# Moving the per-layer input's product from the last stage into the RWKV preparation

## The chip, the core and the metric

One core of a Trainium2 chip runs the whole program. The metric is the device time of one execution in microseconds (us). The profile names the core's engines PE (matrix products; PEld is its weight loads), DVE (vector), ACT (scalar and table functions), POOL (GpSimd) and SP (which here only starts transfers, on the queue the profile calls SPq). On-chip data lies in SBUF, matrix products land in PSUM banks of 128 x 512 numbers, and everything else is in DRAM.

## The reference

One encoder layer over 1024 tokens of width 1024. Only what the change touches is spelled out:

```python
h = rms_norm(x, norm_mix);  proj = h @ w_in            # q, k, v | r, k, v, decay, rate, gate | branch gates
attn = windowed_gqa(q, k, v)                            # 128-token bands
rw = rwkv7_time_mix(...)                                # two scans, forward and backward
x = x + (gate0 * (attn @ w_up_attn) + gate1 * (rw @ w_up_rwkv)) @ w_out
x = x + square(relu(rms_norm(x) @ w_ff1)) @ w_ff2
hp = rms_norm(x, norm_ple)
x = x + (p @ w_ple) * sigmoid(hp @ w_ple_gate)          # p: 1024 x 256, an input
```

`p @ w_ple` needs no result of the layer: `p` (1024 x 256) and `w_ple` (256 x 1024) are both inputs.

## The kernel before

Every fp32 operand of a large product is split into a high part (a rounding cast on ACT, L187) and a low part (the remainder, a subtraction on DVE or POOL, L188), and each product is three matrix instructions: high by high, high by low, low by high (`mm3`, L222; `mm3_steps`, L210, the same one at a time). A weight slab goes through `load_w` (L193): it is loaded in two halves into a staging tile (tag `w_st`, two buffers), each half is cast on ACT, and its remainder is taken on POOL; the parts lie in `w_hi` and `w_lo`, two buffers each.

The stages, in time order:

1. Norm, transposes and the q, k, v columns (to about 105 us). Near its end the transposed keys go to DRAM by POOL's queue (`kT_d`, L362).
2. The RWKV preparation (`with ExitStack() as s1`, L476, about 105 to 375 us). It finishes two column slabs (z12 and z13: decay, rate and gate inputs), and then loops over four pairs of heads `p`. Each turn projects k, r and v (48 matrix instructions each; `shifted`, L510, averages neighbouring tokens: ACT copies, a sum on POOL at L522, a scaled sum on DVE at L523), forms four low-rank products (`lora`, L541, a 128-row and a 64-row instruction for each half), and runs a long DVE and ACT chain to the scan's operands, which go to DRAM at L681 and L682. The "bonus" of turn p is finished by PE during turn p+1 (`add_bonus`, L574): two banks of sums over `rk`, and eight transposes of v. In the last turn the branch gates' products (`gates`, L280) are put between the low-rank products.
3. Attention (about 380 to 510 us), with what is left of the gates as filling. It reads `kT`, which POOL loads from DRAM at L463, ahead of the preparation's first work on POOL.
4. The scan by chunks, the output product, the two feed-forward products in a seven-product scheme (L1448, L1698).
5. The last stage (L1756), over eight tiles of 128 tokens: for each half of 512 columns, six matrix instructions for `p @ w_ple` into one PSUM bank (`pwps`, L1763) and 24 for `hp @ w_ple_gate` into another (`plps`), then a tanh on ACT (L1779) and two DVE instructions (L1780, L1781). During tile k the operands of tile k+1 are made: `p` is loaded, transposed (two instructions) and split; the normed x is transposed (eight instructions) and split.

A planner orders each engine's instructions ahead of the run. It gives the earlier instruction of the program precedence among those whose operands and buffers are free; only the few marked `keep_in_program_order` are tied. A tile takes a buffer of its tag once an earlier tile's last reader is done. On the chip every engine and queue then runs its list in that order.

Of the kernel before, what the change touches and what calls it, by code (L numbers as in the profile page):

```python
# [9 lines left out]
F32 = mybir.dt.float32  # L10
# [127 lines left out]
def block_kernel(ctx: ExitStack, tc: tile.TileContext, I: dict, out: bass.AP):  # L138
# [21 lines left out]
    x1_d = DR.tile([T, DM], F32, name="x1_d")  # L160

    hid_d = {r: DR.tile([FF // P // 2, P, 512], F32, name="hid_" + r) for r in ("A11", "A12", "A22", "S1", "S2", "S3", "S4")}
    kT_d = DR.tile([P, 2, 2, T], F32R, name="kT_d")
    qT_d = DR.tile([NT, P, NH, P], F32R, name="qT_d")
    va_d = DR.tile([T, P], F32, name="va_d")
# [293 lines left out]
            pass  # L459
    sQ.close()  # L460

    kT = PY.tile([P, 2, 2, T], F32R, name="kT", tag="yk")
    nc.gpsimd.dma_start(kT, kT_d)  # L463
    gmask = const("gmask", [P, ND, P])
    pc = G.tile([P, NPC], F32, name="pc")
    nc.sync.dma_start(pc, I["pc"])
# [9 lines left out]
    with ExitStack() as s1:  # L476
# [64 lines left out]
        def lora(d, p, i, bias_col):  # L541

            th = A1.tile([P, T], F32, name="th", bufs=2)
            for h in range(2):
                ps = PX.tile([P, 512], F32, name="px", tag="px", bufs=6)
                cs_, hs = slice(p * P, (p + 1) * P), slice(512 * h, 512 * h + 512)
                nc.tensor.matmul(ps, wlr_h[i][:, d, cs_], lr[i][:, hs], start=True, stop=False)
                nc.tensor.matmul(ps, wlr_l[hrows[i], d, cs_], lr[i][hrows[i], hs], start=False, stop=True)
                nc.scalar.activation(out=th[:, 512 * h:512 * h + 512], in_=ps, func=AF.Tanh, scale=0.5, bias=hb[:, bias_col:bias_col + 1])
            return th  # L550

# [48 lines left out]
        def proj_with(c0, hooks):  # L600
# [9 lines left out]
                    i += 1  # L610
            return pss

        bonus = None
        for p in range(NP):
            if bonus:
                next(bonus)
            kz = shifted(O_RWKV + 512 + p * P, 4 + p)
            rz = shifted(O_RWKV + p * P, p, pin=p > 0)

            kk = A1.tile([P, T], F32, name="kk", bufs=1)  # L620
            ri = A1.tile([P, T], F32, name="ri", tag="sm", bufs=1)
# [17 lines left out]
            for d in range(ND):  # L639
# [33 lines left out]
                nc.vector.scalar_tensor_tensor(out=bk[:, :, bs, :], in0=ch(ta), scalar=0.5, in1=Ei, op0=ALU.mult, op1=ALU.mult)  # L673
                nc.vector.tensor_tensor(out=bk[:, :, ks, :], in0=ch(kd), in1=Ei, op=ALU.mult)
                if d == 0:
                    rk = A1.tile([P, T], F32, name="rk", bufs=1)
                    nc.vector.tensor_scalar_mul(rk, kd, col("r_k", p))
                else:
                    nc.vector.scalar_tensor_tensor(out=rk, in0=kd, scalar=col("r_k", NP + p), in1=rk, op0=ALU.mult, op1=ALU.add)
                    nc.vector.tensor_tensor(out=rk, in0=rk, in1=rz, op=ALU.mult)  # L680
# [952 lines left out]
        nc.vector.tensor_tensor(out=xv, in0=xv, in1=src_, op=ALU.add)  # L1633


    wpv = I["w_ple"].rearrange("(k p) n -> p k n", p=P)
    wgv = I["w_ple_gate"].rearrange("(k p) n -> p k n", p=P)
    wg, loads = [None] * 4, []

# [28 lines left out]
    def ple_load(k):  # L1668
        pt = F2.tile([P, PLE], F32, name="pt", tag="sst", bufs=3)
        nc.sync.dma_start(pt, I["p"][tok(k)[1], :])  # L1670
        return pt

    def ple_p(pt):

        pp = F2.tile([P, 2, 2, P], F32R, name="pp", tag="tmp", bufs=2)
        transpose_split(PH, "acc", pt, lambda q, w: pp[:, 0, q:q + w, :], lambda q, w: pp[:, 1, q:q + w, :], nk=2, bufs=8)
        return pp[:, 0], pp[:, 1]

    def ple_x(xs):

# [5 lines left out]
    for ip, (lr_, rr_, bs, fresh) in enumerate(PRODS):  # L1686
        if fresh:
            banks[bs] = [acc() for _ in range(4)]
        for p in range(NPR):
            if ip == 0 and p < NPRE:  # L1690
                sh, sl, th_, tl_ = pre[p]
            else:
                sh, sl = parts_of(F2, ("sh", "sl"), fetch(F2, hid_d[lr_][p], "sst", 3), NR2)
                th_, tl_ = parts_of(F2, ("th", "tl"), right_of(p, rr_), NR2)
            for i in range(4):
                isl = slice(i * P, (i + 1) * P)
                for j, (x_, y_) in enumerate(((sh, th_), (sh, tl_), (sl, th_))):
                    nc.tensor.matmul(banks[bs][i], x_[:, isl], y_, start=fresh and p + j == 0,  # L1698
                                     stop=p == NPR - 1 and j == 2, skip_group_check=True)
            if ip == 0 and p == NPRE - 1:  # L1700
                sRF.close()
                sFP.close()
                PXX = pool(sX, "x1", side="right")
                X = [PXX.tile([P, 4, DM], F32, name=f"X{e}") for e in range(2)]
                c1 = pool(sC1, "c1", side="right").tile([P, 4, 512], F32, name="c1r")
                t2r = pool(sT2, "t2", side="right").tile([P, NPR, 512], F32, name="t2r")
                t1r = pool(sT1, "t1", side="right").tile([P, NPR, 512], F32, name="t1r")
            if ip == 0 and 0 <= p - (NPR - T1EARLY - NPRE) < NPRE:
                q = p - (NPR - T1EARLY - NPRE)
                nc.sync.dma_start(b11[:, q], w2_block(q, "B11"))  # L1710
            if ip == 0 and p >= NPR - T1EARLY:
                t1_of(p - (NPR - T1EARLY))
            if ip == 1 and p % 2 == 0:
                e, i = divmod(p // 2, 4)
                t = torder[4 * e + i]
                nc.sync.dma_start(X[e][:, i, :], x1_d[t * P:(t + 1) * P, :])
            if ip == 3 and p < 12:
                add_to(*((0, 1), (1, 1), (1, 0))[p // 4], p % 4, c1[:, p % 4])
            if ip > 3 and p % 3 == 1:
                load_next()  # L1720
            if ip == 6:
                if p == 4:
                    pt, xs = ple_load(0), ple_norm(0)
                    ple_scale(0, *xs)
                if p == 9:
                    nxt = [ple_p(pt), ple_x(xs[0])]
        for i in range(4):
            b_ = banks[bs][i]
            if ip == 0:
# [4 lines left out]
        if ip == 3:  # L1734
            sB11.close()
            PLEW = pool(sP, "plew")
            gainp = PLEW.tile([P, DM], F32, name="gainp", bufs=1)
            nc.sync.dma_start(gainp, I["gains"][2:3, :].partition_broadcast(P))
            wp = [PLEW.tile([P, 2, DM], F32R, name=f"wp{i}", bufs=1) for i in range(2)]
            loads += [(wp[0][:, k:k + 1], wp[1][:, k:k + 1], wpv[:, k:k + 1]) for k in range(2)]  # L1740
            ple_gate_w(PLEW, 0)
        if ip == 4:
            sT1.close()
# [7 lines left out]
            PXS = pool(sT2, "plex", bufs=2, side="right")  # L1751
    while loads:
        load_next()


    for k in range(NT):  # L1756
        (pph, ppl), hp = nxt
        nxt = [None, None]
        xv, rows = tok(k)
        for n in range(2):  # L1760
            nsl = slice(512 * n, 512 * n + 512)
            pw = acc(name="pwps")
            mm3(pw, [(pph[:, j, :], ppl[:, j, :], wp[0][:, j, nsl], wp[1][:, j, nsl]) for j in range(2)])  # L1763
            th = F2.tile([P, 512], F32, name="pth", tag="tst", bufs=3)
            ps_ = acc(name="plps")
            steps = mm3_steps(ps_, [(hp[j // 4][0][:, j % 4, :], hp[j // 4][1][:, j % 4, :],
# [1 line left out]
            for m in range(2):  # L1768
                if k + 1 < NT and (n, m) == (0, 0):
                    xs = ple_norm(k + 1)  # L1770
                    pt = ple_load(k + 1)
                    ple_scale(k + 1, *xs)
                if k + 1 < NT and (n, m) == (0, 1):
                    nxt[0] = ple_p(pt)
                if k + 1 < NT and (n, m) == (1, 1):
                    nxt[1] = ple_x(xs[0])
                for _ in range(12):
                    next(steps, None)
            nc.scalar.activation(out=th, in_=ps_, func=AF.Tanh, scale=0.5)  # L1779
# [36 lines left out]
```

## Time and profile before

| | us |
|---|---|
| median of 3 runs | 1818.32 (1815.65 to 1825.78) |
| the profiled execution | 1818.63 |
| its span, first to last instruction | 1816.9 |
| PE busy in the span | 1714.2 (94%) |
| DVE, ACT, POOL busy | 1135.8, 883.1, 321.7 |
| mean granted PE clock | 0.977 of full speed |
| matrix instructions of `p @ w_ple` in the last stage | 96, from 1677.9 us on |
| last instruction of PE | begins at 1811.4 us |

A row of the timeline gives the start, the length, the engine, the line of the kernel, the operation and, in brackets, how long the engine was idle before it and on whom it waited. Matrix instructions overlap, so the step from start to start, not the length, is what one costs. A row of the groups ends with "busy us, mean ns | idle us before, and who ended it".

### The profile page before, as it was taken

What the parts mean: (1) busy time and instruction counts of PE and PEld (TensorE: products, weight loads), DVE (VectorE), ACT (ScalarE), POOL (GpSimd) and SP (SyncE); (2) the same over time, 40 slices, a digit from 0 to 9 for tenths busy, and PEclk for the clock granted to TensorE, in tenths of its full rate; (3) what the DMA queues carried; (4) which work ended last, traced back from release to release, by engine and by line L of the source; (5) the groups of instructions that cost most, each with busy time, mean ns of one, the idle gap of its engine ahead of it and who ended that gap; (6) DMA issues with size and microseconds to landing.
All of it is one profiled execution on the core that took longest, in us unless ns stands there. A gap on an engine that the chain in (4) does not pass through costs nothing. (4 is left out here: it accounts for less than half of the span.)

```text
span 1816.9 us, 29645 instructions
## 1 busy us (share of the span) xinstructions
PE 1714.2 (94%) x11288; PEld 1376.5 (76%) x11288; DVE 1135.8 (63%) x1931; ACT 883.1 (49%) x1624; POOL 321.7 (18%) x265
## 2 busy tenths in 40 slices
PE   7999888989999898988889989999999999999998
PEld 7977666766677777776667867888888888888887
DVE  5646777745845646575564277766766887685442
ACT  5546666547764555455542154544444444454221
POOL 3454544532132112112142000000000000000000
PEclk9999999999999999989999989999999999999999
DMA  5462344674377474576576214444456984574111
GB/s 198 99 183 81 117 145 145 197 202 115 98 201 203 141 196 148 158 199 197 175 225 198 93 47 151 151 152 161 143 163 214 324 262 122 187 221 135 62 41 47
DMA packets 281998, 285.96 MB, mean 157 GB/s; under 512 B 49408, under 2 KB 195712, under 8 KB 281728
## 3 DMA queue, kind: packets, MB, share of 16 engines
q1 hardware_dynamic: 273600, 270.76, 48.3%
q0 software_dynamic: 7824, 12.59, 2.5%
q8 instruction: 89, 1.46, 0.3%
q10 hardware_dynamic: 432, 0.73, 0.1%
q14 instruction: 53, 0.43, 0.1%
HBM read 203.26 MB, written 80.74 MB: 156 GB/s over the span
## 5 line engine op out<-in xcount | busy, mean ns | idle before, releaser
L188 POOL TENSOR_TENSOR wlo<-wst,whi 128x512 fp32r<-128x512 f32 x100 | 149.6, 1508 | 313.1 <-ACT whi L187 262.4
L1698 PE MATMUL ff2ps<-tl,sh 128*128 128x512 f32 x448 | 174.4, 389 | 0.1
L1698 PE MATMUL ff2ps<-th,sl 128*128 128x512 f32 x448 | 174.3, 389 | 0.0
L1698 PE MATMUL ff2ps<-th,sh 128*128 128x512 f32 x448 | 173.9, 389 | 0.0
L175 POOL TENSOR_TENSOR rstd<-ms,neghalf 128x1 f32<-128x1 f32 x24 | 13.3, 554 | 792.9 <-DVE ms L173 792.9
L187 ACT CAST sh<-sst 128x512 fp32r<-128x512 f32 x109 | 67.8, 622 | 99.5 <-PE ff2ps L1698 50.3
L188 DVE TENSOR_TENSOR sl<-sst,sh 128x512 fp32r<-128x512 f32 x109 | 75.1, 689 | 47.4 <-ACT sh L187 47.2
L1698 PEld LDWEIGHTS ff2ps<-tl,sh 128*128 128x128 f32 x448 | 84.1, 188 | 18.2 <-DVE tl L188 0.5
L1698 PEld LDWEIGHTS ff2ps<-th,sh 128*128 128x128 f32 x448 | 84.0, 188 | 17.7 <-ACT th L187 0.3
L1698 PEld LDWEIGHTS ff2ps<-th,sl 128*128 128x128 f32 x448 | 84.1, 188 | 17.5
L187 ACT CAST whi<-wst 128x512 fp32r<-128x512 f32 x100 | 60.7, 619 | 47.5 <-DMA wst<-in_w_in_dram 16.1
L187 ACT CAST w1h<-w1st 128x512 fp32r<-128x512 f32 x48 | 28.5, 621 | 101.1 <-DMA w1st<-in_w_ff_dram 64.1
L188 DVE TENSOR_TENSOR w1l<-w1st,w1h 128x512 fp32r<-128x512 f32 x48 | 31.9, 688 | 52.2 <-ACT w1h L187 52.2
L208 PE MATMUL gps<-rm,bkp 128*128 128x256 f32 x256 | 62.4, 386 | 1.3 <-ACT tm L1061 0.8
L1034 DVE TENSOR_TENSOR gm<-gps,gmask 128x512 f32<-128x512 f32 x64 | 43.7, 685 | 29.5 <-PE gps L208 29.5
L218 PE MATMUL gmm<-hh,wlo 128*128 128x512 f32 x144 | 59.3, 412 | 0.0
L214 PE MATMUL gmm<-hh,whi 128*128 128x512 f32 x144 | 59.2, 411 | 0.0
L216 PE MATMUL gmm<-hl,whi 128*128 128x512 f32 x144 | 59.2, 411 | 0.0
L1086 DVE COPY Wt<-wps 64x512 f32<-64x512 f32 x16 | 10.9, 680 | 71.3 <-PE wps L208 71.3
L208 PEld LDWEIGHTS gps<-rm,bkp 128*128 128x128 f32 x256 | 47.2, 189 | 10.9 <-issue 1.4
L226 PE MATMUL mm<-hh,whi 128*128 128x512 f32 x128 | 51.5, 402 | 3.3 <-ACT z L520 3.3
L188 DVE TENSOR_TENSOR w1l<-ssum,w1h 128x512 fp32r<-128x512 f32 x64 | 43.0, 688 | 16.9 <-ACT w1h L187 16.9
(409 smaller groups left out, 5056.8 us busy)
## 6 DMA issues: line engine op xcount, KB each, us to landing
wst<-in_w_in_dram SPq DMA_DIRECT2D x92, 256.0 KB, 3.5
tst<-in_w_ff_dram SPq DMA_DIRECT2D x80, 256.0 KB, 4.0
w1st<-in_w_ff_dram SPq DMA_DIRECT2D x32, 512.0 KB, 5.2
hid_S<-h SPq DMA_DIRECT2D x64, 256.0 KB, 2.1
sst<-hid_S SPq DMA_DIRECT2D x64, 256.0 KB, 2.8
hid_A<-h SPq DMA_DIRECT2D x48, 256.0 KB, 2.0
sst<-hid_A SPq DMA_DIRECT2D x45, 256.0 KB, 3.9
ra_d<-ra SPq DMA_DIRECT2D x8, 1024.0 KB, 4.5
```

The costliest lines, as they stand in the source:

```text
L175: nc.gpsimd.tensor_tensor(out=r, in0=ms, in1=neghalf.broadcast_to([P, width]), op=ALU.pow)
L187: a = nc.scalar.copy(hi, src)
L188: b = (lo_eng or nc.vector).tensor_tensor(out=lo, in0=src, in1=hi.bitcast(F32), op=ALU.subtract)
L208: tc.keep_in_program_order(nc.tensor.matmul(*a, **kw))
L214: mm(ps, ah, bh, start=(i == 0), stop=False)
L216: mm(ps, ah, bl, start=False, stop=False)
L218: mm(ps, al, bh, start=False, stop=(i == n - 1))
L226: nc.tensor.matmul(ps, ah, bh, start=(i == 0), stop=False)
L1034: nc.vector.tensor_tensor(out=gm[d][:, s % NB, 4 * h:4 * h + 4, :], in0=ps.rearrange("p j q t -> p (j q) t"), in1=gmask[:, d, :].unsqueeze ...
L1086: nc.vector.tensor_copy(Wt[own[0], 0], wp[own[0]])
L1698: nc.tensor.matmul(banks[bs][i], x_[:, isl], y_, start=fresh and p + j == 0, stop=p == NPR - 1 and j == 2, skip_group_check=True)
```

## The change

The product `p @ w_ple` is computed in the preparation, stored to a DRAM tensor `pw_d` and loaded again in the last stage. `ple_in(g)` loads, transposes and splits four tiles of `p`; `ple_product(g, n)` makes four token tiles' half of 512 columns: a slab of `w_ple` through `load_w`, 24 matrix instructions, four copies on ACT, four stores. `ple_in(0)` stands ahead of the loop; two products follow the k and r projections of turn 0, one (with `ple_in(1)`) follows the r projection of turn 1, one that of turn 2. The `p` tiles are staged in `w_st`, the split `p` lies in the buffer of `kT` (tag `yk`), so `kT` is loaded in turn 3; half of the copies go through `gth`, the tag of the bonus sums' second half. To make room, `rk` shares one buffer with `vt` and `bv`. In `lora`, both 128-row instructions now come first, then both 64-row ones.

```diff
+    pw_d = DR.tile([T, DM], F32, name="pw_d")
...
-    kT = PY.tile([P, 2, 2, T], F32R, name="kT", tag="yk")
-    nc.gpsimd.dma_start(kT, kT_d)
...
         def lora(d, p, i, bias_col):
...
-            for h in range(2):
-                ps = PX.tile([P, 512], F32, name="px", tag="px", bufs=6)
-                cs_, hs = slice(p * P, (p + 1) * P), slice(512 * h, 512 * h + 512)
+            pss = [PX.tile([P, 512], F32, name="px", tag="px", bufs=6) for _ in range(2)]
+            for ps, hs in zip(pss, hss):
                 nc.tensor.matmul(ps, wlr_h[i][:, d, cs_], lr[i][:, hs], start=True, stop=False)
+            for ps, hs in zip(pss, hss):
                 nc.tensor.matmul(ps, wlr_l[hrows[i], d, cs_], lr[i][hrows[i], hs], start=False, stop=True)
+            for h, ps in enumerate(pss):
                 nc.scalar.activation(out=th[:, 512 * h:512 * h + 512], in_=ps, func=AF.Tanh, ...)
...
+        pT = PY.tile([P, NT, 2, 2, P], F32R, name="pT", tag="yk")
+        wpv = I["w_ple"].rearrange("(k p) n -> p k n", p=P)
+        def ple_in(g):
+            for i in range(4):
+                t = 4 * g + i
+                pt = PW.tile([P, PLE], F32, name="pt", tag="w_st", bufs=2)
+                nc.sync.dma_start(pt, I["p"][t * P:(t + 1) * P, :])
+                tp = PX.tile([P, 2, P], F32, name="ptp", tag="px", bufs=6)
+                for k in range(2):
+                    nc.tensor.transpose(tp[:, k, :], pt[:, k * P:(k + 1) * P], ident)
+                split(pT[:, t, 0], pT[:, t, 1], tp)
+        def ple_product(g, n):
+            nsl = slice(512 * n, 512 * n + 512)
+            hi, lo = load_w(PW, "w", wpv[:, :, nsl], 512, parts=2)
+            for i in range(4):
+                t = 4 * g + i
+                ps = PX.tile([P, 512], F32, name="pwps", tag="px", bufs=6)
+                mm3(ps, [(pT[:, t, 0, k, :], pT[:, t, 1, k, :], hi[:, k, :], lo[:, k, :]) for k in range(2)])
+                o_ = (A1, PW)[i % 2].tile([P, 512], F32, name="pws", tag=("pws", "gth")[i % 2], bufs=2)
+                nc.scalar.copy(o_, ps)
+                nc.sync.dma_start(pw_d[t * P:(t + 1) * P, nsl], o_)
+        ple_in(0)
...
             kz = shifted(O_RWKV + 512 + p * P, 4 + p)
+            if p == 0:
+                ple_product(0, 0)
             rz = shifted(O_RWKV + p * P, p, pin=p > 0)
+            if p == 0:
+                ple_product(0, 1)
+            elif p < 3:
+                if p == 1:
+                    ple_in(1)
+                ple_product(1, p - 1)
+            else:
+                kT = PY.tile([P, 2, 2, T], F32R, name="kT", tag="yk")
+                nc.gpsimd.dma_start(kT, kT_d)
...
-                    rk = A1.tile([P, T], F32, name="rk", bufs=1)
+                    rk = A1.tile([P, T], F32, name="rk", tag="vt", bufs=1)
...
+    def ple_load(k, n):
+        pw = F2.tile([P, 512], F32, name="pw", tag="sst", bufs=3)
+        nc.sync.dma_start(pw, pw_d[tok(k)[1], 512 * n:512 * n + 512])
+        return pw
...
-            pw = acc(name="pwps")
-            mm3(pw, [(pph[:, j, :], ppl[:, j, :], wp[0][:, j, nsl], wp[1][:, j, nsl]) for j in range(2)])
+            pw = npw
+            if 2 * k + n + 1 < 2 * NT:
+                npw = ple_load(*divmod(2 * k + n + 1, 2))
...
-                if k + 1 < NT and (n, m) == (0, 1):
-                    nxt[0] = ple_p(pt)
```

The old loads of `w_ple` and `p` in the last two stages, and their splits, are gone as well.

More of the change, by code (lines that the diff above doesn't have):

```diff
@@ L543, in lora @@
             th = A1.tile([P, T], F32, name="th", bufs=2)
-            for h in range(2):
-                ps = PX.tile([P, 512], F32, name="px", tag="px", bufs=6)
-                cs_, hs = slice(p * P, (p + 1) * P), slice(512 * h, 512 * h + 512)
+            cs_, hss = slice(p * P, (p + 1) * P), [slice(512 * h, 512 * h + 512) for h in range(2)]
+            pss = [PX.tile([P, 512], F32, name="px", tag="px", bufs=6) for _ in range(2)]
+            for ps, hs in zip(pss, hss):
                 nc.tensor.matmul(ps, wlr_h[i][:, d, cs_], lr[i][:, hs], start=True, stop=False)
+            for ps, hs in zip(pss, hss):
                 nc.tensor.matmul(ps, wlr_l[hrows[i], d, cs_], lr[i][hrows[i], hs], start=False, stop=True)
+            for h, ps in enumerate(pss):
                 nc.scalar.activation(out=th[:, 512 * h:512 * h + 512], in_=ps, func=AF.Tanh, scale=0.5, bias=hb[:, bias_col:bias_col + 1])
@@ L1633, in add_to @@
         nc.vector.tensor_tensor(out=xv, in0=xv, in1=src_, op=ALU.add)
-    wpv = I["w_ple"].rearrange("(k p) n -> p k n", p=P)
     wgv = I["w_ple_gate"].rearrange("(k p) n -> p k n", p=P)
@@ L1666, in ple_scale @@
             nc.vector.scalar_tensor_tensor(out=xs, in0=tok(k)[0], scalar=r, in1=gainp, op0=ALU.mult, op1=ALU.mult))
[L1668 to L1677, printed above, removed]
+    def ple_load(k, n):
+        pw = F2.tile([P, 512], F32, name="pw", tag="sst", bufs=3)
+        nc.sync.dma_start(pw, pw_d[tok(k)[1], 512 * n:512 * n + 512])
+        return pw
     def ple_x(xs):
@@ L1722, in block_kernel @@
                 if p == 4:
-                    pt, xs = ple_load(0), ple_norm(0)
+                    xs = ple_norm(0)
                     ple_scale(0, *xs)
                 if p == 9:
-                    nxt = [ple_p(pt), ple_x(xs[0])]
+                    nxt = ple_x(xs[0])
         for i in range(4):
@@ L1738, in block_kernel @@
             nc.sync.dma_start(gainp, I["gains"][2:3, :].partition_broadcast(P))
-            wp = [PLEW.tile([P, 2, DM], F32R, name=f"wp{i}", bufs=1) for i in range(2)]
-            loads += [(wp[0][:, k:k + 1], wp[1][:, k:k + 1], wpv[:, k:k + 1]) for k in range(2)]
             ple_gate_w(PLEW, 0)
@@ L1753, in block_kernel @@
         load_next()
+    npw = ple_load(0, 0)
     for k in range(NT):
-        (pph, ppl), hp = nxt
-        nxt = [None, None]
+        hp = nxt
         xv, rows = tok(k)
@@ L1770, in block_kernel @@
                     xs = ple_norm(k + 1)
-                    pt = ple_load(k + 1)
                     ple_scale(k + 1, *xs)
-                if k + 1 < NT and (n, m) == (0, 1):
-                    nxt[0] = ple_p(pt)
                 if k + 1 < NT and (n, m) == (1, 1):
-                    nxt[1] = ple_x(xs[0])
+                    nxt = ple_x(xs[0])
                 for _ in range(12):
```

## The prediction

> **What bounds the kernel now.** I read the page's sums, the table of stages, then PE's timeline in the two stages that the edit touches, then the queue of SP.
>
> ```profile
> span 1816.9 us, 29645 instructions
> PE 1714.2 (94%) x11288; PEld 1376.5 (76%) x11288; DVE 1135.8 (63%) x1931; ACT 883.1 (49%) x1624; POOL 321.7 (18%) x265
> ```
>
> PE is busy 94% of the span, so an instruction taken from PE and put elsewhere on PE gains only what it finds idle there. The stages say where that is (engine columns: busy us and instructions; then granted clock, DMA share, GB/s):
>
> ```profile
> core 0: us, PE busy (x) PEld busy (x) DVE busy (x) ACT busy (x) POOL busy (x), PEclk, DMA share, GB/s
> 124.00:152.00 28.00, 24.71 (x100) 19.33 (x99) 17.38 (x18) 12.54 (x21) 12.61 (x9) 0.94 0.40 135
> 191.70:242.60 50.90, 45.81 (x178) 33.98 (x178) 37.69 (x38) 32.13 (x45) 23.14 (x11) 0.93 0.44 135
> 1750.00:1800.00 50.00, 50.00 (x240) 41.59 (x239) 18.51 (x29) 11.70 (x22) 1.10 (x2) 1.00 0.08 32
> ```
>
> In the last stage PE never rests and DVE and ACT are idle more than half the time: PE alone sets it. A turn of the preparation loop (191.7 to 242.6) leaves PE idle for 5.1 us, at a lowered clock.
>
> **Removed from the last stage.** PE's steps near the end:
>
> ```profile
> 1775.53 0.39 PE L226 MATMUL pwps<-wp,pp 128*128 128x512 f32 x1
> ...
> 1776.88 0.39 PE L214 MATMUL plps<-wg,hp 128*128 128x512 f32 x1
> ...
> 1787.34 0.38 PE L249 MATMUL tp<-ident,pt 128*128 128x128 f32 x2
> 1787.47 0.48 PE L214 MATMUL plps<-wg,hp 128*128 128x512 f32 x1
> ```
>
> Six `pwps` take 1776.88 - 1775.53 = 1.35 us. Two transposes of `p` take 0.13 us, and the next instruction 0.48 in place of 0.39: 0.22 us. Per tile 2 x 1.35 + 0.22 = 2.92 us, times eight: **-23.4 us**.
>
> Does something else end last then? The second multiply-add reads only SBUF and costs what the first, which read PSUM, does (mean ns before the last bar), so `pw` from SBUF is free:
>
> ```profile
> L1780 DVE SCALAR_TENSOR_TENSOR pth<-pth,pwps 128x512 f32<-128x512 f32 x16 | 11.0, 686 | 32.2 <-ACT pth L1779 32.2
> L1781 DVE SCALAR_TENSOR_TENSOR X<-pth,X 128x512 f32<-128x512 f32 x16 | 11.1, 692 | 0.6
> wst<-in_w_in_dram SPq DMA_DIRECT2D x92, 256.0 KB, 3.5
> sst<-hid_S SPq DMA_DIRECT2D x64, 256.0 KB, 2.8
> pt<-in_p_dram SPq DMA_DIRECT2D x8, 128.0 KB, 2.0
> ```
>
> Sixteen loads of 256 KB replace eight of 128 KB. Each is asked for one half tile ahead, some 5.9 us (half of a tile's new length, below), and lands in 2.8 (the `sst` row); even behind an output's store, which waits on DVE, it has a whole tile. The thinnest cover is that of the split of the transposed x: it used to hide behind 12 `plps` and 6 `pwps`, and keeps 12 x 0.227 = 2.7 us:
>
> ```profile
> 1705.89 0.87 PE tp L249 x8
> 1720.66 0.87 PE tp L249 x8
> ...
> 1706.36 1.08 ACT L187 CAST hp<-tp 128x512 fp32r<-128x512 f32 x2 [3.92 <-PE tp L249]
> 1706.98 1.29 DVE L188 TENSOR_TENSOR hp<-tp,hp 128x512 fp32r<-128x512 f32 x2 [3.09 <-ACT hp L187]
> ```
>
> By the first two rows, of the chain of waits, a tile takes 14.77 us, and its transposes are over at 1706.76. The split's last half is done at 1706.98 + 1.29 = 1708.27, so 1.5 us are needed, and 1.2 are left. The removed split of `w_ple` lay beside the feed-forward products: nothing.
>
> **Added to the preparation, turn 0.** Two products, 48 instructions at 0.23 us: **+11.0 us** of PE. What idle time do they find?
>
> ```profile
> 125.70 0.56 POOL L463 DMA_DIRECT2D kT<-kT_d  x1 [8.00 <-DMA kT_d<-qkT]
> 126.27 1.91 POOL L522 TENSOR_TENSOR sm<-zr 128x1024 f32<-128x1024 f32 x1
> ...
> 135.41 0.51 PE L226 MATMUL mm<-hh,whi 128*128 128x512 f32 x1 [1.03 <-ACT z L520]
> 143.56 0.50 PE L226 MATMUL mm<-hh,whi 128*128 128x512 f32 x1 [2.26 <-ACT z L520]
> ...
> 145.17 0.63 PE L228 MATMUL mm<-hh,wlo 128*128 128x512 f32 x1
> 145.60 0.63 PE L226 MATMUL mm<-hh,whi 128*128 128x512 f32 x1
> ...
> L839 PE MATMUL sc<-kT,qT x128: 274/337/446, 384.1 to 497.6; 128*128 128x384 f32 x96, 128*128 128x256 f32 x32
> ```
>
> POOL stands 8.0 us at the load of `kT`, which waits for the keys' last store; the neighbour sum of z12 is queued behind it, ACT's and DVE's work on z12 and z13 behind that, and so PE's PSUM banks. PE loses 1.03 + 2.26 us, and eight instructions at steps of 0.43 in place of 0.23 us (1.6 us). The load goes to turn 3 (one slot of 0.56 us on POOL, long before attention's first use at 384.1): the stalls go, **-4.9 us**. But then the two products have no idle time to fill.
>
> Nor is `ple_in(0)` free. Its four tiles use the staging buffers:
>
> ```profile
> SPq L202 <- POOL wlo L188: 129.0, 41, 11.1
> 99.44 2.62 POOL L188 TENSOR_TENSOR wlo<-wst,whi 128x512 fp32r<-128x512 f32 x2
> 100.84 0.37 SPq L202 DMA_DIRECT2D wst<-in_w_in_dram  x1
> 102.08 0.37 SPq L202 DMA_DIRECT2D wst<-in_w_in_dram  x1
> 123.16 0.40 PE L226 MATMUL mm<-hh,whi 128*128 128x512 f32 x1
> 166.89 1.28 DVE L523 SCALAR_TENSOR_TENSOR z<-sm,hmu,z 128x1024 f32<-128x1024 f32 x1 [3.02 <-POOL sm L522]
> 193.84 1.04 PE L583 MATMUL vtp<-ident,z 128*128 128x128 f32 x8
> L187 ACT CAST whi<-wst 128x512 fp32r<-128x512 f32 x100 | 60.7, 619 | 47.5 <-DMA wst<-in_w_in_dram 16.1
> ```
>
> A staging load starts the moment POOL has taken the remainder of the half before. The loads at 100.84 and 102.08 are those of turn 0's k slab, used from 123.16. Now the first two `p` tiles get these buffers, and give them back only when PE has transposed them. PE does that by precedence after z13, at 123.2: the eight transposes of v at 193.84 show it, for their input was ready at 168.2 (the 166.89 row's end) and they stand behind every k and r instruction. Then: two transposes each to 123.6, the other two tiles' load 2.0 us, transposes, the k slab's load 3.5, cast 0.6, remainder 1.3 (half of the 2.62 row): PE starts k about 131, **+7.9 us**, with the eight transposes inside, and a slow start as above, **+1.6**. Bounds: 1.0 us (the transposes alone, if the planner finds PE free earlier) and 11.7 (two of POOL's 1.91 us sums ahead of the remainders).
>
> [...]
>
> **Turn 1.**
>
> ```profile
> 191.74 0.40 PE L214 MATMUL mm<-hh,whi 128*128 128x512 f32 x1
> ...
> 198.41 0.50 PE L569 MATMUL px<-s,one_r 128*128 128x512 f32 x1 [3.53 <-ACT s L187]
> 200.47 0.79 PE L570 MATMUL px<-s,one_r 128*128 128x512 f32 x1 [1.56 <-DVE s L188]
> ```
>
> At each turn's head PE waits 3.53 + 1.56 us for `rk`, and nine slow steps follow (1.8 us): 6.9 us, room for a product (5.5) and four tiles' transposes (1.0). But `ple_in(1)` has the same staging rounds: tiles three and four are loaded after r ends, then the `w_ple` slab, then v's slab: 2.0 + 3.5 + 1.9, product, and v starts some 12 us late, of which 7 lay idle anyway, and the bonus sums no longer wait: **+3 us** (from -1.8, all hidden, to +6). Turn 2 has no `p` tiles: its product fills the gap, the clock stays up, **-1.8** (to +3 if ACT's copies, 0.6 us each as the cast row of their size, and `rk`'s shared buffer push the sums back). Turn 3 keeps its gap.
>
> **Low-rank products.**
>
> ```profile
> 163.08 0.50 PE L548 MATMUL px<-lr,wlrl 64*128 64x512 f32 x1
> 163.51 0.50 PE L547 MATMUL px<-lr,wlrh 128*128 128x512 f32 x1
> ```
>
> Alternating row counts cost 0.43 a step. Four now have two changes of count instead of four: 4 x 0.43 less 2 x 0.20 if equal neighbours run at 0.23 (64-row neighbours are not in this trace: 0.23 to 0.43). That is 0.4 us, 1.6 a turn. In turns 0 to 2 it goes into PE's wait for `rk`; in turn 3, full of gates, I count half: **-0.8** (0 to -6.4).
>
> **The sum**, on the profiled execution's 1818.63 (0.3 above the median 1818.32): -23.4 + 11.0 - 4.9 + 7.9 + 1.6 + 3 - 1.8 - 0.8 = -7.4, so **1811 us**.
>
> **Rivals.** (A) *Smooth staging*: the `p` tiles find PE free early, as nothing but precedence keeps them back. Without the 9.5, plus 1.0 for transposes, and with turn 1 at -1.8: -20.7, **1798**. Against it: the vtp row. (B) *Half*: one of the two stalls only, say turn 0's at half price and turn 1 at zero: **1804**. (C) *The last stage doesn't shorten in full*: if ACT's tanh, queued in front of the cast, makes the x split late by 1 us more than its cover, seven tiles lose about 1 each: **1818**. (D) *Slower*: SP's list now has 16 stores that each wait for an ACT copy, with weight loads queued behind them. If each of the four products thus puts one unhidden staging round into PE's stream (3.5 + 0.6 + 1.3 = 5.4 us), that is +22: **1833**. It decides from 1.9 us a product. For it: SP's row above, one wait of 11.1 us; against it: ACT is idle 19 of 51 us in a turn.
>
> **Chances.** Forecast 0.42, A 0.20, B 0.17, C 0.11, D 0.10. About 0.5% (9 us) is what a measurement tells from no change. Faster than 1809: A, most of B, and a quarter of the forecast, 0.46; slower than 1827: nearly all of D, 0.09; within: 0.45. Range 1797 to 1825: leaves out D and the lower edge of A. The forecast's own range: 1805 to 1817.
>
> **What would show it.** Right: a period of 11.8 us (14.77 before) between transposes in the last stage; no POOL wait at `kT` near 120; k of turn 0 starting near 131 behind two load rounds; its `p` loads on SP ahead of the k slab's; the next turn's head without a wait for `rk`. Wrong: k starting near 123 to 125 (A), transposes in the last stage followed by PE waiting on DVE (C), or PE waiting on POOL's remainders in every product (D).

## The result, and the profile after

The changed kernel takes 1833.39 us (median of 4 runs, 1833.04 to 1833.89), the kernel before 1819.55 (4 runs beside them): a ratio of 1.0083, interval 1.0059 to 1.0107. It is slower by 0.8%, where the forecast was 1811 and its range ended at 1825.

The page's sums and the table of stages of the changed kernel (its line numbers are up to 39 higher than before):

```profile
span 1831.3 us, 29762 instructions
PE 1712.2 (93%) x11288; PEld 1375.6 (75%) x11288; DVE 1132.6 (62%) x1929; ACT 894.5 (49%) x1646; POOL 332.3 (18%) x273
...
207.50:258.40 50.90, 41.74 (x167) 30.79 (x166) 28.91 (x33) 31.48 (x49) 19.59 (x11) 0.90 0.48 151
1750.00:1800.00 50.00, 50.00 (x242) 41.76 (x241) 23.00 (x34) 13.57 (x26) 2.20 (x4) 1.00 0.25 90
```

PE's work is the same (1712.2 us busy, 1714.2 before), but the span is 14.4 us longer: PE waits more. The last stage still has PE busy in all of its 50 us. The 50.9 us from r's end in turn 1 on (207.5) hold 41.7 us of PE, where they held 45.8 before (from 191.7).

The last stage gained what was forecast. In the chain of waits, two tiles' transposes follow each other by 11.79 us (14.77 before). The second multiply-add, from the groups of DVE's instructions, waits for next to nothing (0.5 us in all). The whole stage, from the transposes of the first tile (the first row of PE's timeline before, then after) to the start of the last product, takes 110.9 us (1714.4 to 1825.3) where it took 134.3 (1677.1 to 1811.4): -23.4.

```profile
1752.27 0.87 PE tp L250 x8
1764.06 0.87 PE tp L250 x8
...
L1810 DVE SCALAR_TENSOR_TENSOR X<-pth,X 128x512 f32<-128x512 f32 x16 | 11.1, 692 | 0.5
...
1677.12 1.03 PE L249 MATMUL tp<-ident,xs 128*128 128x128 f32 x8
...
1714.44 1.04 PE L250 MATMUL tp<-ident,xs 128*128 128x128 f32 x8
...
L219 PE MATMUL plps<-wg,hp x128: 388/389/398, 1716.7 to 1825.3; 128*128 128x512 f32 x128
```

The loss is in the preparation. PE's timeline there, with the first low-rank product of each of the four turns (`px<-lr`), the first score of attention (`sc`), and, in brackets, those of PE's long waits that are new in turns 0 to 2:

```profile
125.19 0.99 PE L625 MATMUL ptp<-ident,pt 128*128 128x128 f32 x4 [1.95 <-DMA pt<-in_p_dram]
132.50 0.80 PE L227 MATMUL mm<-hh,whi 128*128 128x512 f32 x1 [6.31 <-ACT whi L188]
...
179.67 0.63 PE L546 MATMUL px<-lr,wlrh 128*128 128x512 f32 x2
...
213.43 1.12 PE L625 MATMUL ptp<-ident,pt 128*128 128x128 f32 x4 [5.33 <-DMA pt<-in_p_dram]
217.50 1.65 PE L227 MATMUL pwps<-whi,pT 128*128 128x512 f32 x3 [2.96 <-ACT whi L188]
...
240.29 0.63 PE L546 MATMUL px<-lr,wlrh 128*128 128x512 f32 x2
...
279.07 0.80 PE L215 MATMUL mm<-hh,whi 128*128 128x512 f32 x1 [4.55 <-ACT whi L188]
...
295.35 0.80 PE L570 MATMUL px<-s2h,one_r 128*128 128x512 f32 x1 [4.89 <-ACT s2h L188]
...
303.23 0.63 PE L546 MATMUL px<-lr,wlrh 128*128 128x512 f32 x2
354.21 0.63 PE L546 MATMUL px<-lr,wlrh 128*128 128x512 f32 x2
421.45 1.19 PE L878 MATMUL sc<-kT,qT 128*128 128x256 f32 x4 [3.67 <-DMA qT<-qT_d]
```

The same marks in the kernel before (its first `sc` stands in the prediction, 384.1):

```profile
162.76 0.40 PE L547 MATMUL px<-lr,wlrh 128*128 128x512 f32 x1
...
213.59 0.40 PE L547 MATMUL px<-lr,wlrh 128*128 128x512 f32 x1
...
264.58 0.40 PE L547 MATMUL px<-lr,wlrh 128*128 128x512 f32 x1
...
315.68 0.40 PE L547 MATMUL px<-lr,wlrh 128*128 128x512 f32 x1
```

These marks cut the preparation into five stages: from the last step of z13 (122.93 before, 122.41 after) to turn 0's mark, from mark to mark, and from turn 3's mark to `sc`. "Turn 1" below is the stretch from turn 0's mark to turn 1's. A stage is a difference inside one trace; the start of the preparation itself moves by up to 4 us between traces of kernels that don't differ ahead of it (z13's last step: 122.1 to 126.1).

| us | turn 0 | turn 1 | turn 2 | turn 3 | to `sc` | sum |
|---|---|---|---|---|---|---|
| before | 39.8 | 50.8 | 51.0 | 51.1 | 68.4 | 261.1 |
| after | 57.3 | 60.6 | 62.9 | 51.0 | 67.2 | 299.0 |
| difference | +17.4 | +9.8 | +12.0 | -0.1 | -1.1 | +37.9 |
| forecast | +15.6 | +3 | -1.8 | -0.8 with the next | | +16.0 |

The preparation's +37.9 and the last stage's -23.4 make 14.5. The preparation starts 0.5 us earlier, the stretch from `sc` to the last stage is the same to 0.1 us (1293.0 after, 1293.1 before), and what follows the last product is 0.5 us longer: 14.4. In some of the kernels that follow, that stretch is longer by up to 11 us (1304.3), for reasons that were not looked into, so a total is not read as the preparation's.

By the table of stages over the five stretches, PE is busy 256.9 us in place of 237.0 and idle 42.2 us in place of 24.1. In sum the moved work filled no idle time; it brought 18 us of new idle time with it.

Turn 0 is right, turns 1 and 2 are not: the forecast had PE's wait of 5.1 us for `rk` as room for a product. After, that wait is gone in turns 1 and 2, and others stand there.

Four views of the changed kernel show what PE waited for in turn 2. ACT's timeline:

```profile
274.78 1.15 ACT L662 ACTIVATE sq<-z,pc 128x1024 f32<-128x1024 f32 x1 [8.52 <-DVE z L522]
...
276.30 0.62 ACT L188 CAST s<-rk 128x512 fp32r<-128x512 f32 x1
...
278.39 1.15 ACT L188 CAST whi<-wst 128x512 fp32r<-128x512 f32 x2
...
292.35 0.62 ACT L188 CAST whi<-wst 128x512 fp32r<-128x512 f32 x1 [5.32 <-DMA wst<-in_w_in_dram]
294.68 0.62 ACT L188 CAST s2h<-sq 128x512 fp32r<-128x512 f32 x1 [1.71 <-DMA pw_d<-pws]
```

The queue of SP:

```profile
268.38 1.31 SPq L203 DMA_DIRECT2D wst<-in_w_in_dram  x1
...
272.84 1.15 SPq L203 DMA_DIRECT2D wst<-in_w_in_dram  x1
...
280.73 0.37 SPq L203 DMA_DIRECT2D wst<-in_w_in_dram  x1
...
282.94 0.37 SPq L203 DMA_DIRECT2D wst<-in_w_in_dram  x1
...
286.57 2.96 SPq L638 DMA_DIRECT2D pw_d<-pws  x2
```

POOL's timeline:

```profile
282.87 0.62 POOL L657 DMA_DIRECT2D kT<-kT_d  x1
```

And the landing times (the last number, us) of 240 to 300 us, against that of `v_d` from 205 to 235 (third row), then those of SP's loads of 280.73 and 282.94 alone:

```profile
kT<-kT_d POOLq DMA_DIRECT2D x1, 2048.0 KB, 9.7
...
v_d<-vt SPq DMA_DIRECT2D x1, 512.0 KB, 8.4
...
v_d<-vt SPq DMA_DIRECT2D x1, 512.0 KB, 4.2
...
wst<-in_w_in_dram SPq DMA_DIRECT2D x1, 256.0 KB, 3.0
...
wst<-in_w_in_dram SPq DMA_DIRECT2D x1, 256.0 KB, 9.4
```

First, v's slab. Its two loads are issued at 268.38 and 272.84 and take 4.9 and 5.0 us to land, so the first half lies ready at 273.3. ACT casts it at 278.39, because on ACT's list the casts stand behind the square of k and the casts of `rk`, and those wait 8.52 us for DVE's chain. That is the very chain for which PE used to wait. Before, the slabs of k, r and v alternated in two buffers, and v's was cast while r ran (in turn 1 at 184.97; r ended at 191.7). With the product's slab between them v's comes one place later, into the buffer that r holds.

Second, `s2h`, the high part of the norm's squares, which PE sums. On ACT's list it stands behind a cast (292.35) that waits 5.32 us for its load. SP issued that load at 282.94, 0.07 us behind POOL's load of `kT` (2 MB, 282.87), and it took 9.4 us to land; the load of 280.73 took 3.0. Then `s2h` waits itself for a store, that of 286.57, which took 8.0 us, since the output copies share its buffers. The store of `v_d` took 8.4 us, and DVE waits 7.26 us for the buffer that it frees. All three are under way while `kT`'s load is (282.87 to 292.57).

### The profile page after: what moved, and what is told of

Same layout as the page of the kernel before. It is cut to its first block, busy times and chain, and to the rows that moved or that the text cites. A ratio compares the mean times of both kernels' runs of the same rounds, so it can differ in the third digit from the quotient of the medians.

```text
span 1831.3 us, 29762 instructions
## 1 busy us (share of the span) xinstructions
PE 1712.2 (93%) x11288; PEld 1375.6 (75%) x11288; DVE 1132.6 (62%) x1929; ACT 894.5 (49%) x1646; POOL 332.3 (18%) x273
## 3 DMA queue, kind: packets, MB, share of 16 engines
q1 hardware_dynamic: 279072, 280.20, 49.7%
## 5 line engine op out<-in xcount | busy, mean ns | idle before, releaser
L189 POOL TENSOR_TENSOR wlo<-wst,whi 128x512 fp32r<-128x512 f32 x108 | 159.1, 1485 | 324.7 <-ACT whi L188 275.3
L188 ACT CAST sh<-sst 128x512 fp32r<-128x512 f32 x109 | 67.8, 622 | 110.8 <-PE ff2ps L1731 53.5
L188 ACT CAST whi<-wst 128x512 fp32r<-128x512 f32 x108 | 65.8, 619 | 64.2 <-DMA wst<-in_w_in_dram 35.7
L215 PE MATMUL gmm<-hh,whi 128*128 128x512 f32 x144 | 58.6, 407 | 0.7 <-ACT whi L188 0.5
L217 PE MATMUL gmm<-hl,whi 128*128 128x512 f32 x144 | 58.3, 405 | 0.0
L209 PEld LDWEIGHTS gps<-rm,bkp 128*128 128x128 f32 x256 | 47.8, 192 | 12.5 <-issue 2.7
L1125 DVE COPY Wt<-wps 64x512 f32<-64x512 f32 x16 | 10.9, 680 | 74.0 <-PE wps L209 74.0
```

The source lines that it names most:

```text
L188: a = nc.scalar.copy(hi, src)
L189: b = (lo_eng or nc.vector).tensor_tensor(out=lo, in0=src, in1=hi.bitcast(F32), op=ALU.subtract)
L209: tc.keep_in_program_order(nc.tensor.matmul(*a, **kw))
L215: mm(ps, ah, bh, start=(i == 0), stop=False)
L217: mm(ps, ah, bl, start=False, stop=False)
```

## Experiments

The theories. S: the excess is the staging rounds of the p tiles. G: the output copies share buffers with the sums. Q: stores on SP's list hold up weight loads (the prediction's rival D as it was put). O: the wait for `rk` is room for a product's matmuls, but its inputs and outputs, and v's slab, go over ACT's list behind the chain. P: there is no room; a product costs its 5.5 us wherever it stands. K: `kT`'s load holds back the stores. All ratios are to the kernel before.

**Three parts alone.** First the copies in buffers of their own:

```diff
-  o_ = (A1, PW)[i % 2].tile(..., tag=("pws", "gth")[i % 2], bufs=2)
+  o_ = A1.tile([P, 512], F32, name="pws", tag="pws", bufs=2)
```

> The changed kernel, but the four copies of each product's output rotate through two buffers of their own instead of alternating with the buffers that also hold the halves of the sums (s2h, s2l). Theory G (the shared buffers): the sums' half s2h of turns 1 and 2 no longer waits for a store of pw_d to land, so the PE waits of 0.86 and 4.89 us before px go, and about eight slow steps behind the second (1.6 us): 1833 - 7 = 1826. Theory Q (SP's list, rival D as put: stores that wait for ACT's copies hold the weight loads behind them): those stores are still there, and the third copy now waits for the first store: 1833 to 1836. Theory S (the staging rounds of the p tiles are the whole of the excess): 1833.

1837.31 us, ratio 1.011 [1.0092, 1.0129]. PE's waits of 0.86 and 4.89 us for `s2h` are gone and turn 2 falls from 62.9 to 59.5, but turn 3 grows from 51.0 to 57.8: DVE stands 7.84 us at `bv` until a store of `v_d` lands. G's wait was real, its removal gave nothing: the lateness moved to the next buffer that is freed by a store. (1837 lies past every time that was expected; Q's 1833 to 1836 is the nearest.)

Next the p tiles by pairs:

```diff
-  pt = PW.tile([P, PLE], F32, name="pt", tag="w_st", bufs=2)
+  pt = A1.tile([P, 2, PLE], F32, name="pt", tag="pws", bufs=2)   # two tiles a load
```

> The changed kernel, but the p tiles are loaded two at a time into the two buffers of the outputs' copies, so that they take no staging buffer of the weights and need no second round. Theory S: k of turn 0 starts near 124.5 us instead of 132.50 (its waits of 1.95 and 6.31 us nearly gone), the waits of 5.33 and 2.96 us in turn 1 go, with the slow steps behind them (1.6 us each): 1833 - 18 = 1815. Theory O (ACT's list: v's slab is cast behind work that waits for DVE's chain, as in turn 2, where it costs 4.55 + 0.46 us): turn 1 gets that stall in place of the one removed, 1820. Theory Q (stores on SP's list): nothing in these buffers changes for it, 1830 or more.

1829.83 us, 1.0053 [1.0028, 1.0078]. Turn 0 falls by 10.0 us to 47.3 (expected 8 and 1.6): S holds there. Turn 1 does not move (60.9): the rounds of 5.33 + 2.96 us go, and one wait takes their place. PE's and ACT's rows of this run:

```profile
207.25 0.79 PE L227 MATMUL pwps<-whi,pT 128*128 128x512 f32 x1 [7.92 <-ACT pT L188]
```

```profile
203.69 1.15 ACT L664 ACTIVATE sq<-z,pc 128x1024 f32<-128x1024 f32 x1 [8.52 <-DVE z L522]
...
206.83 1.19 ACT L188 CAST pT<-ptp 128x256 fp32r<-128x256 f32 x4
```

The tiles were in place early (PE transposed them at 198.29); their casts stood behind the chain on ACT's list. In turn 1 the staging was only the first of two causes. The time itself, 1830, is the one that Q expected; it is the rows that speak for O.

Then the gain alone, without the preparation's part:

```diff
-        ple_in(0)
-                ple_product(0, 0)   # and the other three, and ple_in(1)
-  nc.sync.dma_start(pw, pw_d[...])
+  nc.sync.dma_start(pw, x1_d[...])
```

> The changed kernel with the p tiles' transposes and the four products left out of the preparation; the last stage adds rows of another array in DRAM, so the outputs are not the reference's. It has the shorter last stage, the later load of kT and the low-rank products in parts alone. Expected if the three gains stand in full: 1819.6 - 23.4 - 4.9 - 4.7 (1.2 us in each of four turns, by the changed kernel's stages) = 1787, and the changed kernel less this is what the preparation pays, 46 us. If part of the last stage's gain is lost at its end, or kT's wait comes back at another place: 1792 or more.

1795.42 us, 0.9878 [0.9858, 0.9898]. The last stage's products, from PE's group of them:

```profile
L219 PE MATMUL plps<-wg,hp x128: 388/389/398, 1681.4 to 1790.0; 128*128 128x512 f32 x128
```

From the first tile's transposes (1679.1) it is 110.9 us to the last of them, 134.3 before: -23.4, in full. The preparation takes 261.9 us, 261.1 before: the load of `kT` and the low-rank order brought nothing. So the preparation pays 1833.4 - 1795.4 = 38 us in the changed kernel, for work that took 23.4 us in the last stage.

Last of these, the two small parts on the kernel before:

```diff
-    nc.gpsimd.dma_start(kT, kT_d)       # ahead of the preparation
+            if p == 3:                  # in turn 3; the low-rank products by part, too
+                nc.gpsimd.dma_start(kT, kT_d)
```

> The kernel before with two parts of the edit alone: kT is loaded in turn 3, and the low-rank products are ordered by part. If both are gains on PE's stream as the changed kernel's stages say: 1819.6 - 4.9 - 4.7 = 1810. If the prediction's smaller price for the order holds (its 1.6 us a turn swallowed by the wait for rk in turns 0 to 2, half counted in turn 3): 1819.6 - 4.9 - 0.8 = 1814. If kT's wait only moves to another place: 1819.

1816.33 us, 0.9991 [0.9976, 1.0006]: no gain. POOL's timeline says why:

```profile
126.54 0.56 POOL L622 DMA_DIRECT2D kT<-kT_d  x1 [8.70 <-DMA kT_d<-qkT]
127.11 1.91 POOL L520 TENSOR_TENSOR sm<-zr 128x1024 f32<-128x1024 f32 x1
```

The planner put the load back where it stood; only pT's hold on its buffer makes it late in the changed kernel. The low-rank order shortens each turn's products (the stretch from the mark to v's transposes is 29.9 us, 31.1 before), and PE then waits 4.74 us for `rk` instead of 3.53.

**Is it ACT's list?** The second group's tiles were moved to turn 0 (with the pairs):

```diff
                 ple_product(0, 1)
+                ple_in(1)
...
-                if p == 1:
-                    ple_in(1)
```

> The kernel with paired p tiles, and also the second group's tiles are loaded, transposed and cast in turn 0, right behind the second product. Theory O (ACT's list: what the turn's head casts stands behind the square of k and the casts of rk, which wait for DVE's chain): the 7.92 us that turn 1's product waited for its pT casts go, but v's slab, still cast behind that chain, stops PE for 4.5 to 5.5 us as in turn 2; some 3 us less than paired p tiles alone, 1827. If the product's own inputs were all that was late: 7.9 + 1.6 less, 1820. Theory S (staging rounds): nothing is left to gain, 1830.

1826.56 us, 1.0039 [1.0016, 1.0062]; turn 1 56.2 (60.9 with pairs alone), and PE waits 4.35 us for v's slab there, 4.55 in turn 2. O's 1827.

Then the product's weights left the slabs' rotation:

```diff
+        ykb = PY.tile([P, 2, 2, T], F32R, name="ykb", tag="yk")   # half: pT of one group
-            hi, lo = load_w(PW, "w", wpv[:, :, nsl], 512, parts=2)
+            hi, lo = wph, wpl                                       # other half of ykb
```

> As the last, and the product's weights no longer rotate through the two slabs that k, r and v use: pT holds one group of four tiles, and the slab of w_ple lies in the other half of that buffer. So v's slab takes the buffer that k leaves, is cast during r, ahead of the chain in ACT's list, as in the kernel before. Theory O: the waits for v's slab in turns 1 and 2 (4.5 + 0.5 us and more) go, the two products fill the wait for rk; a turn takes about 51 us as without products, where it took 61 to 63; what is left are the waits of the sums for pw_d's stores (1.4 and 3.6 us with paired p tiles): 1808, and 1802 if those go too. Theory Q (stores on SP's list in front of weight loads): the same 16 stores are on the list, v's loads still come late, 1820 or more. If each product costs PE its 5.5 us wherever it stands: 1815 to 1820.

1828.55 us, 1.0067 [1.004, 1.0094]. No wait for v's slab is left in either turn, with all 16 stores still on SP's list: O, against Q. Yet the time is nowhere near O's 1808 (it lies in the range that Q expected), for the sum stands where it was: turn 0 is 6 us longer (its product waits 2.74 us for its weights), turn 1 takes 54.0, turn 2 63.6 with waits of 2.81 (a PSUM bank that ACT empties late), 3.58 and 4.60 (`s2h`).

> As the last, with the four copies of a product's output in two buffers of their own. If the sums' half then waits for no store: 1802. If, as in the run with these buffers alone, the later copies wait for the first store to land and something else becomes late: 1808 to 1812.

The same with own output buffers: 1826.16 us, 1.0049 [1.0029, 1.0068]. Turns 1 and 2 take 54.3 and 54.3, turn 3 58.4, with 8.46 us of DVE at `bv`. Again turn 3 pays, and neither expected time came.

**The load of `kT`, held late, on the kernel before.**

```diff
+                tc.keep_in_program_order(nc.gpsimd.dma_start(kT, kT_d))   # p == 3
```

> The kernel before, with the load of kT held at its place in turn 3 of POOL's list (where the edit's line alone was moved, the planner put it back ahead of z12's neighbour sum, and POOL waited 8.70 us at it as before). If kT's load causes the waits of 1.03 and 2.26 us and the slow steps behind them: 1819.6 - 4.9 = 1814.7. If they have another cause (PSUM banks freed by ACT behind DVE's work on z12): 1819.

1817.75 us, 1.0 [0.9976, 1.0024]. The table of stages of this run:

```profile
124.00:158.50 34.50, 34.50 (x151) 28.15 (x150) 19.12 (x22) 19.02 (x28) 15.02 (x9) 1.00 0.26 77
158.50:163.50 5.00, 5.00 (x13) 2.03 (x11) 1.98 (x2) 5.00 (x9) 3.38 (x2) 1.00 0.19 52
164.00:172.00 8.00, 8.00 (x17) 4.86 (x17) 8.00 (x5) 3.18 (x4) 6.13 (x2) 0.50 0.11 33
```

PE no longer waits in turn 0, which is 5.5 us shorter (34.4): the load did cause those waits, at about the forecast's price (4.9). The next turn takes 54.5 instead of 50.8, part of it at a granted clock of 0.50 (third row), and by `sc` all is given back.

**PE's part of a product, and the rest.** Two kernels with the weights apart, in which turns 1 and 2 multiply what turn 0 left:

```diff
+            for k in range(2 if g == 0 else 0):     # no slab of w_ple for group 1
-                ple_in(1)
+                if g == 0:                          # copies and stores: first kernel only
```

> The kernel with the product's weights apart, but the products of turns 1 and 2 are 24 matmuls each on the operands that the products of turn 0 left (no p tiles of the second group, no slab of w_ple, no copies of the output, no stores); the last stage reads the first group's rows twice, so the outputs are not the reference's. It prices PE's part alone. Theory O (the wait for rk is room for a product, and what costs is the work for it on ACT's list): the low-rank products of turns 1, 2 and 3 start 51 us apart as without products, and only turn 0's two products are paid: no_prep's 1795.4 and 8 to 10, 1804. Rival P (the turn is a loop of PE and the chain on ACT and DVE, in which a product costs its 5.5 us wherever it stands): 56 us apart, 1815.

> As the last, with the copies of the outputs on ACT and the stores on SP's list back; still no p tiles of the second group and no slab of w_ple, so the outputs are not the reference's. The difference to the last run is the price of copies and stores. Theory O: ACT's eight copies of 0.6 us stand in the chain's way and the sums' half waits for stores: 8 to 12 us more, 1814. Theory Q (stores on SP's list in front of v's loads): the same sum, but PE then waits for v's slab. Rival P: no difference, 1815.

1818.4 us, 1.0005 [0.9989, 1.0022], and 1829.28, 1.0064 [1.004, 1.0087]. By its time the first looks like P. By stages it does not: turn 1 takes 49.7 us with 24 matmuls more than the 50.8 without; the product is free there. Turn 2 takes 53.2, and turn 3 58.6, where DVE, POOL and SP show:

```profile
281.26 1.29 DVE L589 TENSOR_TENSOR bv<-px,z 128x512 f32<-128x512 f32 x2 [9.41 <-DMA v_d<-vt]
```

```profile
269.50 0.62 POOL L664 DMA_DIRECT2D kT<-kT_d  x1
```

```profile
270.04 0.46 SPq L586 DMA_DIRECT2D v_d<-vt  x1
```

The store of `v_d` starts half a microsecond behind `kT`'s 2 MB; DVE needs its buffer, and the sums that make `kk` are queued behind. Copies and stores cost another 10.9 us by the total (expected 8 to 12), but only 6.6 us by the marks: turns 1 and 2 take 55.1 and 62.1, with 8.64 us for `s2h`, whose store of `pw_d` lands beside `kT`'s load (272.08) here, while turn 3 is back at 50.8.

> The whole work, the product's weights apart and own buffers for the output's copies, with these copies on DVE in place of ACT. Theory O: some 2.2 us of each product leave ACT's list, 1826 - 6 = 1820. If DVE, on which the chain to rk runs for most of a turn, is as full: 1826 or more.

Copies on DVE (`nc.vector.tensor_copy`): 1819.99 us, 1.0021 [1.0002, 1.0041], the expected 1820. The stages don't show the expected way, though: turns 1 to 3 take 57.2, 58.2 and 54.8, together 3 us more than with the copies on ACT, and the profiled execution took 1826.9. I do not count it as support.

**`kT` in pieces, and all causes together.**

```diff
-                nc.gpsimd.dma_start(kT, kT_d)
+                if p == NP - 1:   # four times, between the steps of the two directions
+                    tc.keep_in_program_order(nc.gpsimd.dma_start(kT[:, d, 0], kT_d[:, d, 0]))
```

> The changed kernel, but kT is loaded in four pieces, held at their places on POOL's list between the steps of turn 3's two directions, instead of in one piece that the planner puts at the head of turn 3's work, 282.9 us. Theory K (that load holds back the stores of pw_d and v_d that start within 4 us of it, 8 to 11 us to land in place of 2 to 3): the wait of 4.89 us before the sums of turn 2 shrinks to the 0.9 of turn 1, its slow steps go, and DVE's wait of 7.3 us at bv with them: 1833 - 6 = 1827. If the stores are late for their place on SP's list alone: 1833. If the pieces only move the collision into turn 3, where the gates' weights are loaded: 1831 to 1834.

1836.45 us, 1.009 [1.007, 1.0109]. PE's row in turn 2:

```profile
297.06 0.50 PE L570 MATMUL px<-s2h,one_r 128*128 128x512 f32 x1 [1.71 <-ACT s2h L188]
```

4.89 became 1.71, DVE's wait at `bv` 7.26 became 4.30, the store of `v_d` landed in 4.6 us in place of 8.4, and turn 2 takes 57.4 in place of 62.9: K holds. The pieces collide elsewhere: turn 3 takes 1.3 us more and the stretch to `sc` 3.3, with waits for the gates' weights; turns 0 and 1 take 1.2 us more. The preparation stands at 299.3, and the time is no lower: the last of the three expectations, 2 us past its end.

> The whole work with each cause taken away: p tiles in pairs outside the staging buffers, the second group's at the head of turn 1; group 0's weights through the slabs, group 1's in the half of pT's buffer that one group leaves, with both parts of their split on POOL; output copies in two buffers of their own, on ACT; kT in four pieces in turn 3. Theory O with K: the low-rank products of turn 0 start near 171 as with paired p tiles, turns 1 to 3 take 52 to 53, 52 to 53 and 51 us, so attention starts near 394, 27 us before the changed kernel: 1806. If two products cost their 5.5 us anyway: 1815. If POOL's list becomes late with two more passes: 1820.

> As the last, with the second group's output copies on DVE, so that ACT's list in turn 2 is that of the kernel without products. Theory O: ACT's 2.2 us of copies stood in front of the square and the sums: 2 to 4 us less than the last. If DVE's chain takes their place: 2 to 4 us more.

1822.03 us, 1.0022 [1.0004, 1.004], and 1820.27, 1.0009 [0.9994, 1.0024]. Turn 0 is 46.2 in both; turns 1 to 3 take 56.4, 54.5, 57.6 and 58.3, 59.1, 51.8. PE waits 2.1 and 4.4 us for PSUM banks, as was expected for a late POOL list. That POOL is the cause was not tried by itself. Turn 3's 57.6 in the first has the look of turn 3 in the runs with own buffers and in the one with PE's part alone. DVE stands at `bv`:

```profile
282.42 1.29 DVE L589 TENSOR_TENSOR bv<-px,z 128x512 f32<-128x512 f32 x2 [5.56 <-DMA v_d<-vt]
```

So `kk` comes 5.3 us behind the mark that begins turn 3, where the kernel before has it 0.2 us ahead of the mark. In `own_out`, `own_w_out` and `pe_only` it comes 5.7, 7.1 and 7.0 us behind, and turn 3 is longer than before by 6.7, 7.3 and 7.5 us (6.5 here). In this run no piece of `kT` is near (the first starts at 352.8), so `kT` is not all that makes this store late; SP issued it at 276.84, right behind two stores of `pw_d`. One part of the edit is in every run with the products: `rk` shares the one buffer of `vt` and `bv`. No run undid it, so its share in these waits stays open.

Last, the work that must be done in turns 1 and 2 was cut: turn 0's second slab is kept for turn 1's product, and the second group's tiles come behind v of turn 0. `kT`'s four pieces come in turn 2 (not in the diff below), the tiles by pairs, and the copies have buffers of their own.

```diff
+  hi, lo = load_w(...) if (g, n) == (0, 0) else (wph, wpl)
+  for k in range(2 if (g, n) in ((0, 1), (1, 0)) else 0):    # (1, 1) loads nothing
-  ple_product(1, p - 1)
+  ple_product(1, 2 - p)
+  if p == 0: ple_in(1)          # behind v of turn 0; kept_w_head: at the head of turn 1
```

> The whole work. The second half of w_ple's columns stays where turn 0's second product left it, in the half of pT's buffer, and turn 1's product uses it again, so that only turn 2's product loads and splits a slab; the second group's p tiles are loaded, transposed and cast behind v of turn 0; outputs in own buffers; kT in four pieces in turn 2's two directions. ACT's list in turn 1 is that of the kernel without products but for the four copies. Theory O with K: low-rank products of turn 0 near 172, then turns of 51 to 52, 53 to 54 and 52 us, attention near 397: 1808, under the kernel before. If POOL's and ACT's remaining passes still make PE wait for its PSUM banks by 2 to 4 us a turn: 1814 to 1820. If the pieces of kT delay turn 2's stores: turn 3's head as late as with one piece, 1818.

> As the last, but the second group's p tiles come at the head of turn 1, where their four casts stand between the exponentials of turn 0's second direction. If casts among the chain's work cost as in the runs before (PE waits 2.1 us for z's PSUM bank): 2 to 4 us more than the last. If not: the same.

1810.4 us, 0.9949 [0.9931, 0.9966], and 1806.9, 0.9942 [0.9923, 0.9962]: both are faster than the kernel before, with intervals wholly below 1. PE's and ACT's timelines of the first:

```profile
207.94 0.51 PE L570 MATMUL px<-s,one_r 128*128 128x512 f32 x1
...
250.25 0.50 PE L227 MATMUL mm<-hh,whi 128*128 128x512 f32 x1 [2.77 <-ACT z L519]
```

```profile
239.74 1.15 ACT L188 CAST ykb<-wst 128x512 fp32r<-128x512 f32 x2
...
249.53 0.66 ACT L519 ACTIVATE z<-mm,omm 128x512 f32<-128x512 f32 x1
```

Turn 1, whose product needs no slab, takes 49.3 us and PE meets `rk` without a wait: that is the forecast's picture of a filled gap. Turn 2, whose product does, takes 58.5; ACT casts the slab at 239.74 among the chain's work, and PE waits for a PSUM bank behind it. The preparation costs 273.6 - 261.1 = 12.5 us, and -23.4 + 12.5 = -10.9; measured were -10.2 (1820.6 for the kernel before beside it). Against the run with all causes apart the preparation is 11.2 us shorter; turn 1 gives 7.1 us of that, but turn 3 and the stretch to `sc` give 8.9 and turn 2 takes 4.0, and the place of `kT`'s pieces changed there too. What the kept slab alone is worth was not tried. The second kernel's time can't be told from the first's; in its stages turn 1 takes 53.5 with the casts at its head, and turn 2 55.3.

## Why the prediction was wrong

- **Last stage, -23.4.** Right: -23.4. Rival C (feed of the x split) did not come.
- **Turn 0, +15.6 in sum.** Right in size (+17.4) and in its main cause: k starts at 132.50 (forecast 131), behind two load rounds, and pairs of p tiles give it back. The stalls of the term -4.9 are gone too, because pT holds the load's buffer; moving the line alone moves nothing, the planner puts it back. Held late by itself the load shortens turn 0 by 5.5 us and the whole by nothing. What the term left out is the load's new place: it was priced at "one slot of 0.56 us on POOL" in turn 3, and the 9.7 us in which its 2 MB land at nothing. It started in turn 2, beside that turn's loads and stores.
- **Turn 1, +3.** Mis-sized: +9.8. The two staging rounds were seen and the start of v forecast 12 us late; it came 17.9 late (225.34 in place of 207.49, PE's timeline). The 7 us that were set against it are not free: what fills them needs ACT, and ACT's list has the chain ahead of it.
- **Turn 2, -1.8.** This is the step that failed: "Turn 2 has no `p` tiles: its product fills the gap, the clock stays up". The matmuls do fill it (no wait ahead of them), but the gap reappears behind them as 4.55 us for v's slab and 4.89 for `s2h`, and the granted clock of the turn is 0.89, where it was 0.93. Its upper bound, +3 "if ACT's copies ... and rk's shared buffer push the sums back", looked at the right engine with too small a mechanism: not 0.6 us a copy, but the place in an in-order list behind an 8.5 us wait, and a load and a store that have to land while 2 MB are under way (9.4 and 8.0 us here). Turns 1 and 2 miss by 6.8 + 13.8 = 20.6 of the 22 us.
- **Low-rank order, -0.8.** 1.2 us a turn (1.6 in the forecast), taken by the wait for `rk`, as said; -1.2 in turn 3 and behind it, and alone no gain that can be told from none.
- **Rival D, 1833.** Its number came by luck, its mechanism hardly. The staging rounds that PE sees, 6.31 us in turn 0 and 5.33 + 2.96 us in turn 1, are those of the `p` tiles; no product of turn 0 waits for one, and the first half of v's slab in turn 2 had been asked for in time. SP's stores did hold up a load, that of 289.63, but nothing waited for it. D was given 0.10, and what stood against it was "ACT is idle 19 of 51 us in a turn". That was the error in weighing: 8.5 us of ACT's idle time were one wait in its list, not room.
- **The clock.** In the run with `kT` held late PE has no idle time at all from 124 to 163.5, then a granted clock of 0.50 from 164 to 172. So a low clock came there without a wait of PE ahead of it: the prediction's slow steps (1.6 us in turn 0, 1.8 at a turn's head) stand behind waits alone.

## What to carry to other kernels

A gap on the bounding engine is only room for work whose inputs don't pass the thing the gap waits for. Before counting a gap as filled, go down the in-order lists of the engines that cast, copy and load for the new work, and ask what stands ahead of each; idle time of such an engine can be one wait at the head of its list, as the 8.5 us of ACT's were here. Ask also what a transfer that gets a new place will run beside. Judge an edit by differences between marks inside one trace: a total can hide one stage that gained and the next that paid.

## What the runs showed of the hardware

- A granted clock of 0.50 without idle time before it: in the run with `kT` held late it follows 5 us of low-rank products with alternating row counts (13 instructions in 5.00 us, second row of its table above), and lasts until 173.5, 10 us, with PE busy throughout. In the kernel before, the same products (162.76 to 167.81) are followed by steps of 0.23 us, at a granted clock of 1.00 from 170 to 180. What brings the low clock about was not tried.
- Beside `kT`'s 2 MB load, issued by POOL, transfers issued by SP landed late: a store of `v_d` took 8.4 us, where it took 4.2 in turn 1 and 4.6 with the load elsewhere, and a 256 KB weight load 9.4 us, where the one 2.2 us ahead of it took 3.0. While the load was under way (282.87 to 292.57), its queue took 54.5% of the 16 engines' time and SP's queue 38.6%: another queue was no shelter here.
- In the changed kernel the neighbouring 128-row low-rank products ran at the plain step (0.23 us): the rows of two show 0.63 us for both (179.67), a step of 0.24 in front of the 0.39 of one. From the first pair of 64-row products on (180.23 to 182.87) the pairs follow each other by 0.66 us. With a step of about 0.23 inside a pair (0.73 us for two, 0.50 for one) that leaves 0.43 for the change of the row count.
